# A two-layer SSD and DeltaNet trunk on one core: a list of units with three entries moved, and small weights loaded in another order

## The chip, the cores and the metric

The kernel runs on one core of one Trainium2 chip. The metric is device time in microseconds (us) of one execution, lower is better. Besides, one execution is recorded by the hardware profiler; its times are the ones that rows and views show.

The core has a matrix engine (PE, whose weight loads stand apart as PEld), a vector engine (DVE), a scalar engine for activations (ACT), GpSimd (POOL) and a queue that issues DMAs (SP). Each runs its own instructions in the order in which they stand. One waits for another through semaphores.

## The reference, cut to what matters

Two layers. Each is a SwiGLU feed-forward block at half weight, a mixing block, and a second feed-forward block; all are float32, on 256 tokens of width 1024. The mixing block is what the change touches:

```
u = rms_norm(h, mix_norm[l])
(z_s, xbc, dt_s, qkv, z_d, b_d, a_d, gate_s, gate_d) = jnp.split(u @ w_in[l], split_points, axis=-1)
y_s = mamba2_branch(z_s, xbc, dt_s, ...)        # 32 heads of 64 channels in 4 groups, chunks of 128 tokens
y_d = deltanet_branch(qkv, z_d, b_d, a_d, ...)  # 8 heads of 128 channels, chunks of 64 tokens
merged = (sigmoid(gate_s) * (y_s @ ssm_w_branch[l]) + sigmoid(gate_d) * (y_d @ dn_w_branch[l]))
h = h + merged @ w_out[l]
```

In the Mamba branch, per group of 8 heads, with `xs` the convolved and activated input, `dt` a softplus and `a_cum` a running sum of `dt * a`:

```
xdt    = xs * dt
y_diag = (C B^T * exp(a_cum[l] - a_cum[s]) * causal) @ xdt      # decay products, inside a chunk
y_off  = C @ state_in * exp(a_cum)                              # from the chunk before
yg     = (y_diag + y_off + xs * D) * silu(z)
y      = yg * rsqrt(mean(yg^2) + eps) * ssm_norm                # mean over the group's 512 channels
```

## The kernel before, in words

**Weights.** All large weights stream through one path. A slab of 128x1024 float32 (`wraw`, 5 buffers, 512 KB) is loaded by SP, rounded to a high half by ACT (`whi`, line 68) and subtracted to a low half by DVE (`wlo`, line 71); 5 buffers hold each half. Every product is three matmuls: high by high, high by low, low by high. A buffer comes free when the last matmul on it is done, so ACT's next `whi` waits for PE, and SP's next load waits for DVE's `wlo`. `take()` hands out the next slab and makes the preparations five ahead.

**The mixing block.** `mixer` computes units in the order of the list `ORDER` (line 46); the stream of weights is laid out in DRAM in the same order. `x20` is the first and `x21` the second half of the third group's input (48 matmuls of 128x256 into a PSUM bank `xs`; then a convolution: one ACT multiply and three DVE taps `ca` for each half bank, and an ACT SiLU into `xsT`). For group g, `Dg` makes the decay matrix (`dc`: a DMA, two DVE steps, an ACT exponential, a DVE multiply); `Sg`, the first part of `ssd(g)`, transposes `xsT` on PE (8 transposes into two banks `xsb`) and makes five state inputs on DVE (`xD`, `xdt` for each chunk, and `xe`); `Tg`, the second part, makes the decay products on PE (`ydb`, 64 small matmuls, and `yob`) and then on DVE adds and gates them (`xD`, `yo`, `yz`), sums squares on ACT (`jk`, into `sss`), takes the power -1/2 on POOL (`srr`) and scales `yz` on ACT. `g` units are gates (`t` banks, 128x512 matmuls). `N` is the DeltaNet branch product `branch("d", 4, ...)`: 96 matmuls of 128x512 into four banks `b`; for each pair of heads `dn_T` transposes into a bank `oT`, multiplies on DVE (`og`), and splits into `bh` (ACT) and `bl` (DVE). `o` is the first such pair, made ahead. `y` is the first transpose (`yT`) of the Mamba branch.

**PSUM.** The pool `trp` has four banks, taken in turn by `xsb`, `oT`, `ydb`, `yob`, `yT` and other short work; the pool `accp` has four, taken in turn by `xs`, `t`, `b`. Where a tile takes a bank, its first matmul waits for the last reader of the tile that had the bank before.

**The order on each engine** is made when the program is built: units are written out in the order of `ORDER`, and a scheduler places instructions of neighbouring units among one another. It is fixed from then on.

**The start of the mixing block.** While the feed-forward block ends, SP loads three small tensors: `lp` (convolution weights), `rp` (biases and decay rates) and `wsr` (weights of 48 scalar channels), and the norm vector `nw` of the next block. `wsr` is split into `wsc` on ACT and DVE; 17 matmuls on it give `psm`, which ACT copies to `smT` and PE transposes into `pst`. `ea` is an exponential of the decay rates, on ACT; it needs a table load when the table in use is another.

Of the kernel before, what the change touches and what calls it, by code (L numbers as in the profile page):

```python
# [7 lines left out]
F32 = mybir.dt.float32  # L8
F32R = mybir.dt.float32r
I32 = mybir.dt.int32  # L10
AF = mybir.ActivationFunctionType
ALU = mybir.AluOpType
# [4 lines left out]
P = 128  # L17
# [5 lines left out]
KT = D // P  # L23
# [3 lines left out]
RPW = 112  # L27
# [18 lines left out]
ORDER = """  # L46
z20 s z10 z11 s z21 s M k1 k0 q1 k2 k3 K1 K0 q3 q0 K3 K2 v0 q2 I Q0 I Q3 I z30 v1 z31 Q2 v2 V0 I v3
V1 I V3 I Q1 V2 d0 R R R b3 R b2 b0 R b1 R d2 R x00 R d1 x01 R d3 R R P R g100 g101 D0 S0 x10 T0 D1
x11 g110 g111 S1 x20 T1 o x21 N D2 y S2 D3 x30 x31 T2 g000 g010 g001 S3 g011 T3
""".split()  # L50


# [1 line left out]
def trunk_kernel(ctx, tc, x, wst, wsm, norms, lpar, rpar, cst, out):  # L54
    nc = tc.nc
    V, A, G, PE = nc.vector, nc.scalar, nc.gpsimd, nc.tensor

    cpool = ctx.enter_context(tc.tile_pool(name="cpool", bufs=1))
    wpool = ctx.enter_context(tc.tile_pool(name="wpool", bufs=1))
    slots = ctx.enter_context(tc.tile_pool(name="slots", bufs=1))  # L60
    s2 = ctx.enter_context(tc.tile_pool(name="s2", bufs=9))
# [5 lines left out]
    def act(o, i, func=AF.Copy, **kw):  # L67
        return A.activation(out=o, in_=i, func=func, **kw)  # L68

    def tt(o, a, b, op):  # L70
        return V.tensor_tensor(out=o, in0=a, in1=b, op=op)  # L71

    def stt(o, a, s, b, op0, op1):
        return V.scalar_tensor_tensor(out=o, in0=a, scalar=s, in1=b, op0=op0, op1=op1)

    def ts(o, a, s1, op0, sc2=None, op1=None):
        if op1 is None:
            return V.tensor_scalar(out=o, in0=a, scalar1=s1, scalar2=None, op0=op0)
        return V.tensor_scalar(out=o, in0=a, scalar1=s1, scalar2=sc2, op0=op0, op1=op1)
# [4 lines left out]
    def tmp2(name):  # L84
        return s2.tile([P, 512], F32, tag="s2", name=name)

    def trb(name):
        return trp.tile([P, 512], F32, tag="tr", name=name)
# [4 lines left out]
    def small(shape, name, bufs=2):  # L93
        return sm.tile(shape, F32, tag=name, name=name, bufs=bufs)
# [54 lines left out]
    state = {"loaded": 0, "prepped": 0, "taken": 0, "last": None, "hold": False, "behind": {}, "late": {}, "first": 0, "turns": {}, "first_chunk": False, "cap": n_forms}  # L149
# [62 lines left out]
    def norm_vec(i):  # L212
        nw = cpool.tile([P, D], F32, tag="nw", name="nw")
        with tc.issue_after(state["last"].ins):
            nc.sync.dma_start(nw[:], norms[i].partition_broadcast(P))
        return [nw[:, n * 512 : (n + 1) * 512] for n in range(2)]
# [375 lines left out]

    def mixer(l, nxt):
        with tc.issue_after(state["last"].ins):
            lp = cpool.tile([P, LPW], F32, tag="lp", name="lp")
            nc.sync.dma_start(lp[:], lpar[l])
            rp = cpool.tile([P, RPW], F32, tag="rp", name="rp")
            nc.sync.dma_start(rp[:], rpar[l].partition_broadcast(P))
            wsr = s2.tile([P, KT, 48], F32, tag="s2", name="wsr")
            nc.sync.dma_start(wsr[:], wsm[l])  # L600
        snw = lp[:, 240:256]
        dnw = lp[:, 256:257]
        alog = rp[:, 40:80]
# [47 lines left out]
        def scalars():  # L651
            psm = trb("psm")
            for kt in range(KT):
                both = wsc[:, kt].rearrange("p o c -> p (o c)")
                if kt < KT - 1:
                    PE.matmul(psm[0:96, 0:S], both, uTh[:, kt, :], start=kt == 0, stop=False)
                PE.matmul(psm[0:48, 0:S], wsc[:, kt, 0], uTl[:, kt, :], start=False, stop=False)
                if kt == KT - 1:
                    PE.matmul(psm[0:96, 0:S], both, uTh[:, kt, :], start=False, stop=True)
            smT = s2.tile([96, S], F32, tag="s2", name="smT")  # L660
            act(smT[:], psm[0:96, 0:S])
            pst = trb("pst")
            for t in range(2):
                PE.transpose(pst[:, t * 96 : (t + 1) * 96], smT[:, t * P : (t + 1) * P], ident[0:96, 0:96])
            pv2 = pst[:, 0:192].rearrange("p (t o c) -> p t o c", t=2, o=2)
            pvs = small([P, 2, 48], "pvs", 1)
            pv = pvs[:]
            act(pv, pv2[:, :, 1])
            tt(pv, pv2[:, :, 0], pv, ALU.add)
            scr = s2.tile([P, 5, 2, 40], F32, tag="s2", name="scr")  # L670
            xb, ax, z, s_, q_ = (scr[:, i] for i in range(5))
            tt(xb, pv[:, :, 0:40], rp[:, None, 0:40].to_broadcast([P, 2, 40]), ALU.add)
            act(dq[:, :, 8:16], pv[:, :, 40:48], AF.Tanh, scale=0.5)
            ts(dq[:, :, 8:16], dq[:, :, 8:16], 0.5, ALU.mult, 0.5, ALU.add)
            ea = small([P, 40], "ea", 1)
            with tc.issue_after(state["input"][0].ins):
                act(ea[:], alog, AF.Exp)
            stt(ax, xb, -1.0, xb, ALU.mult, ALU.max)
            act(z, ax, AF.Exp, scale=-1.0)
            ts(s_, z, 2.0, ALU.add)  # L680
            V.reciprocal(out=s_, in_=s_)
            tt(s_, s_, z, ALU.mult)
            tt(q_, s_, s_, ALU.mult)
            ts(z, q_, 1.0 / 15.0, ALU.mult)
            for d_ in (13.0, 11.0, 9.0, 7.0, 5.0, 3.0):
                stt(z, z, 1.0 / d_, q_, ALU.add, ALU.mult)
            stt(z, z, 1.0, s_, ALU.add, ALU.mult)
            ts(ax, xb, 0.0, ALU.max)
            stt(sp[:], z, 2.0, ax, ALU.mult, ALU.add)
            stt(la[:], sp[:], -1.0, ea[:, None, :].to_broadcast([P, 2, 40]), ALU.mult, ALU.mult)  # L690
            yield
            psr = trb("psr")
            for t in range(2):
                PE.matmul(psr[0:40, t * 256 : (t + 1) * 256], la[:, t, :], UU, start=True, stop=True)
            pr = psr[:].rearrange("p (t c) -> p t c", t=2)
            V.tensor_copy(rows[0:32], pr[0:32, :, 0:P])
            V.tensor_copy(rows[32:40], pr[32:40, :, P : 2 * P])
            nc.sync.dma_start(rdram[:], rows[:].rearrange("p t c -> p (t c)"))
            pac = trb("pac")
            for t in range(2):  # L700
                PE.transpose(pac[:, t * 40 : (t + 1) * 40], rows[:, t, :], ident[0:40, 0:40])
            V.tensor_copy(ac[:], pac[:, 0:80].rearrange("p (t c) -> p t c", t=2))
            V.tensor_copy(dq[:, :, 0:8], ac[:, :, 32:40])
            yield
            psp = trb("psp")
            for c in range(4):
                PE.matmul(psp[:, c * 16 : (c + 1) * 16], SEL[c % 2], dq[:, c // 2, :], start=True, stop=True)
            for a in range(2):
                V.tensor_copy(
                    pq[64 * a : 64 * a + 64].rearrange("p k h c -> p c k h"),  # L710
                    psp[64 * a : 64 * a + 64, 0:64].rearrange("p (c k h a) -> p c k h a", c=4, k=2, h=4)[:, :, :, :, a],
                )
# [484 lines left out]
        def dn_branch():  # L1197
            ps = branch("d", 4, dn_T)
            m = tg[1]
            for t in range(2):  # L1200
                for n in range(2):
                    sl = slice(n * 512, (n + 1) * 512)
                    stt(m[:, t, sl], m[:, t, sl], 1.0, ps[t][n][:], ALU.add, ALU.mult)

        sc, inv, rc = scalars(), invert(), recur()
        units = {"k": k_unit, "q": q_unit, "v": v_unit}
        rests, heads = {}, {}
# [73 lines left out]
    norm_first(nw0)  # L1281
    for l in range(DEPTH):
        ffn(norm_vec(3 * l + 1))
        mixer(l, norm_vec(3 * l + 2))
        add = ffn(norm_vec(3 * l + 3) if l + 1 < DEPTH else None)
    nw = norm_vec(3 * DEPTH)
    for t in range(2):
# [3 lines left out]
        o = tmp2("fo"), tmp2("fo")  # L1291
# [7 lines left out]
        z = small([P, 2], "zz")  # L1299
# [139 lines left out]
```

## Time and profile before

| what | us |
|---|---|
| time, median of 3 runs (1545.19 to 1546.01) | 1545.27 |
| time of the profiled execution | 1543.84 |
| its span, first to last instruction | 1542.1 |
| PE busy | 1525.1 |
| PEld busy | 1385.3 |
| DVE busy | 1229.8 |
| ACT busy | 949.8 |
| POOL busy | 82.6 |
| layer 1: `z20` to the end of the mixing block | about 202 to 594 |
| layer 2: the same | about 964 to 1355 |

A row of a timeline reads: start, duration, engine, line, operation, output and inputs, shape, count, and in brackets how long the engine had been idle and what ended that. Matmul durations are modelled and overlap, so the starts of neighbouring matmuls tell more than durations: a 128x512 matmul begins about 0.23 us after the one before, a 128x256 about 0.117 us. Rows of the chain of waits give start, duration and what. Rows of the waits give the wait's total, its number and the longest.

### The profile page before, as it was taken

To read this page: it belongs to the slowest core of one execution; us is meant where nothing else is said; L and a number is where in the kernel's file an instruction comes from. 1 tells how busy PE (TensorE), PEld (TensorE's weight loads), DVE (VectorE), ACT (ScalarE), POOL (GpSimd) and SP (SyncE) were. 2 spreads that over 40 slices of the span, in tenths; PEclk is the share of its full clock that TensorE was granted. 3 is DMA by queue.
4 is the path that set the end of the run, shared out by engine and by line. 5 is a ranking of instruction groups with operands and counts; after the bars stand their busy time and mean duration, and the time that the engine had idled before them with its cause. 6 is when DMAs were issued, how large, how long until landed. Compare 5 with 4: busy or idle time off the path is not lost.

```text
span 1542.1 us, 29082 instructions
## 1 busy us (share of the span) xinstructions
PE 1525.1 (99%) x11473; PEld 1385.3 (90%) x11473; DVE 1229.8 (80%) x1859; ACT 949.8 (62%) x1536; POOL 82.6 (5%) x92
## 2 busy tenths in 40 slices
PE   8999999999999999999999999999999999999998
PEld 7999879999988888999899998899998888899997
DVE  5878768967899766789778887689579996678886
ACT  5656667766665645566555566776756666455565
POOL 0000010000000000000100012010000000000010
PEclk9999999999999999999999999999999999999999
DMA  7687765553565556577866687566346555556775
GB/s 272 187 266 227 232 223 174 183 164 112 180 209 172 157 174 191 184 252 217 264 221 227 204 254 238 182 196 186 117 137 204 180 167 187 175 179 191 250 241 156
DMA packets 98831, 305.73 MB, mean 198 GB/s; under 512 B 22837, under 2 KB 23813, under 8 KB 97670
## 3 DMA queue, kind: packets, MB, share of 16 engines
q1 hardware_dynamic: 93796, 290.95, 57.1%
q0 software_dynamic: 4608, 12.58, 5.0%
q8 instruction: 90, 1.47, 0.4%
q14 instruction: 47, 0.39, 0.1%
q10 hardware_dynamic: 290, 0.33, 0.1%
HBM read 297.72 MB, written 1.92 MB: 194 GB/s over the span
## 4 chain that ended last, share of the span: by engine, by line
PE 90%; DVE 3%; ACT 3%; DMA 2%; issue 1%; POOL 0%; SPq 0%; POOLq 0%; ACTq 0%; DVEq 0%
PE fc L346 10%; PE fc L340 9%; PE fc L345 9%; PE t L366 9%; PE o L337 4%; PE o L336 4%; PE o L335 4%; PE f L366 3%; PE b L337 3%; PE b L335 3%; PE b L336 3%; PE p L336 2%; PE p L335 2%; PE p L337 2%; PE xs L340 1%; PE xs L345 1%
## 5 line engine op out<-in xcount | busy, mean ns | idle before, releaser
L71 DVE TENSOR_TENSOR wlo<-wraw,whi 128x1024 fp32r<-128x1024 f32 x488 | 592.2, 1222 | 189.9 <-ACT whi L68 175.4
L68 ACT ACTIVATE whi<-wraw 128x1024 fp32r<-128x1024 f32 x488 | 511.4, 1059 | 266.8 <-PE fc L345 87.3
L346 PE MATMUL fc<-uW,wlo 128*128 128x256 f32 x1280 | 354.9, 277 | 0.0
L340 PE MATMUL fc<-uW,whi 128*128 128x256 f32 x1280 | 354.1, 277 | 0.0
L345 PE MATMUL fc<-uW,whi 128*128 128x256 f32 x1260 | 348.3, 276 | 0.0
L340 PEld LDWEIGHTS fc<-uW,whi 128*128 128x128 f32 x1280 | 240.5, 188 | 0.8
L346 PEld LDWEIGHTS fc<-uW,wlo 128*128 128x128 f32 x1280 | 240.5, 188 | 0.0
L345 PEld LDWEIGHTS fc<-uW,whi 128*128 128x128 f32 x1260 | 236.5, 188 | 0.8
L366 PE MATMUL t<-whi,uW 128*128 128x512 f32 x512 | 165.4, 397 | 0.0
L366 PEld LDWEIGHTS t<-whi,uW 128*128 128x128 f32 x512 | 95.9, 188 | 21.6 <-issue 1.3
L68 ACT ACTIVATE whi<-wsum 128x1024 fp32r<-128x1024 f32 x64 | 68.0, 1062 | 58.7 <-PE fc L345 32.3
L366 PE MATMUL t<-wlo,uW 128*128 128x512 f32 x256 | 100.1, 392 | 0.0
L71 DVE TENSOR_TENSOR wlo<-wsum,whi 128x1024 fp32r<-128x1024 f32 x64 | 78.2, 1222 | 8.3 <-ACT whi L68 5.9
L335 PE MATMUL b<-whi,bh 128*128 128x512 f32 x192 | 76.1, 398 | 0.3 <-ACT bh L68 0.2
L336 PE MATMUL b<-wlo,bh 128*128 128x512 f32 x192 | 75.0, 390 | 0.0
L337 PE MATMUL b<-whi,bl 128*128 128x512 f32 x192 | 74.3, 394 | 0.3 <-DVE bl L71 0.3
L340 PE MATMUL xs<-uW,whi 128*128 128x256 f32 x256 | 72.8, 284 | 0.0
L346 PE MATMUL xs<-uW,wlo 128*128 128x256 f32 x256 | 71.4, 279 | 0.0
L345 PE MATMUL xs<-uW,whi 128*128 128x256 f32 x254 | 70.5, 278 | 0.0
L335 PE MATMUL o<-whi,gh 128*128 128x512 f32 (+1 forms) x160 | 62.0, 388 | 0.0
L337 PE MATMUL o<-whi,gl 128*128 128x512 f32 (+1 forms) x160 | 61.8, 386 | 0.0
L336 PE MATMUL o<-wlo,gh 128*128 128x512 f32 (+1 forms) x160 | 61.7, 386 | 0.0
(337 smaller groups left out, 3301.2 us busy)
## 6 DMA issues: line engine op xcount, KB each, us to landing
wraw<-in_wst_dram SPq DMA_DIRECT2D x504, 512.0 KB, 4.8
wsum<-in_wst_dram SPq DMA_DIRECT2D x16, 512.0 KB, 7.3
wsum<-in_wst_dram POOLq DMA_DIRECT2D x16, 512.0 KB, 8.6
dc<-rdram SPq DMA_DIRECT2D x8, 1024.0 KB, 8.6
nw<-in_norms_dram SPq DMA_DIRECT2D x6, 512.0 KB, 5.3
h<-u POOLq DMA_DIRECT2D x12, 256.0 KB, 6.4
gb<-rdram SPq DMA_DIRECT2D x8, 256.0 KB, 6.1
h<-in_x_dram SPq DMA_DIRECT2D x4, 256.0 KB, 3.7
```

What stands on the lines that cost most here:

```text
L68: return A.activation(out=o, in_=i, func=func, **kw)
L71: return V.tensor_tensor(out=o, in0=a, in1=b, op=op)
L335: PE.matmul(ps, lh, rh, start=start, stop=False)
L336: PE.matmul(ps, lh, rl, start=False, stop=False)
L337: return PE.matmul(ps, ll, rh, start=False, stop=stop)
L340: PE.matmul(ps, wh, mh, start=start, stop=False)
L345: PE.matmul(ps, wh, ml, start=False, stop=False)
L346: PE.matmul(ps, wl, mh, start=False, stop=stop)
L366: ins = PE.matmul(ps[t][:], st, mv, start=k0 == 0 and j == 0, stop=k0 == KT - 2 and j == 5)
```

## The change

Two places. In `ORDER` the unit `x20` moves ahead of `S1`, and `T1` moves behind `x21`; the weight stream in DRAM follows. In `mixer` the small loads change: `wsr` comes first and lies in the slot `y3` rather than in one of nine short-lived buffers, then `rp`, `lp`, and the norm vector last; and `ea` is placed behind another exponential, `z`, of the same table.

```
 ORDER = """
 ...
 V1 I V3 I Q1 V2 d0 R R R b3 R b2 b0 R b1 R d2 R x00 R d1 x01 R d3 R R P R g100 g101 D0 S0 x10 T0 D1
-x11 g110 g111 S1 x20 T1 o x21 N D2 y S2 D3 x30 x31 T2 g000 g010 g001 S3 g011 T3
+x11 g110 g111 x20 S1 o x21 T1 N D2 y S2 D3 x30 x31 T2 g000 g010 g001 S3 g011 T3
 """.split()
...
     def mixer(l, nxt):
         with tc.issue_after(state["last"].ins):
+            wsr = slots.tile([P, KT, 48], F32, tag="y3", name="wsr")
+            nc.sync.dma_start(wsr[:], wsm[l])
+            rp = cpool.tile([P, RPW], F32, tag="rp", name="rp")
+            nc.sync.dma_start(rp[:], rpar[l].partition_broadcast(P))
             lp = cpool.tile([P, LPW], F32, tag="lp", name="lp")
             nc.sync.dma_start(lp[:], lpar[l])
-            rp = cpool.tile([P, RPW], F32, tag="rp", name="rp")
-            nc.sync.dma_start(rp[:], rpar[l].partition_broadcast(P))
-            wsr = s2.tile([P, KT, 48], F32, tag="s2", name="wsr")
-            nc.sync.dma_start(wsr[:], wsm[l])
+        nxt = norm_vec(nxt)
...
             ea = small([P, 40], "ea", 1)
-            with tc.issue_after(state["input"][0].ins):
+            stt(ax, xb, -1.0, xb, ALU.mult, ALU.max)
+            with tc.issue_after(act(z, ax, AF.Exp, scale=-1.0).ins):
                 act(ea[:], alog, AF.Exp)
-            stt(ax, xb, -1.0, xb, ALU.mult, ALU.max)
-            act(z, ax, AF.Exp, scale=-1.0)
...
-        mixer(l, norm_vec(3 * l + 2))
+        mixer(l, 3 * l + 2)
```

The places that the prediction speaks of, as the instructions stand. First ACT at the start of the mixing block, before (-) and now (+):

```order
 L68 ACTIVATE uW<-hnT 128x4x128 x2
+L68 ACTIVATE wsc<-wsr 128x8x48
 L68 ACTIVATE yz<-t_2180 128x512
-L68 ACTIVATE whi<-wraw 128x1024
-L68 ACTIVATE wsc<-wsr 128x8x48
-L68 ACTIVATE whi<-wraw 128x1024
-L68 ACT_TABLE_LOAD
-L68 ACTIVATE ea<-rp 128x40
-L68 ACTIVATE whi<-wraw 128x1024
-L68 ACT_TABLE_LOAD
+L68 ACTIVATE whi<-wraw 128x1024 x3
```

The split of the small weights moved ahead of the first gate and of three roundings, and `ea` left with two table loads (it stands some rows later, behind another exponential, with none).

Second, PE in the DeltaNet branch as it stands now, from the end of the third bank's part for the first pair of heads (`oT_5620` and `oT_5667` are the third and fourth pair, `xsb_5771` group 2, `bh_5439` the first pair, `bh_5580` the second):

```order
L337 MATMUL b_5571<-whi_5347,bl_5440 128x512
L1154 MATMUL oT_5620<-cs_79,vb_2285 128x2x64 x4
L1154 MATMUL oT_5667<-cs_79,vb_2285 128x2x64 x4
L1169 MATMUL yT_5760<-cs_79,yz_2179 128x128 x4
L335 MATMUL b_5572<-whi_5341,bh_5439 128x512
L336 MATMUL b_5572<-wlo_5342,bh_5439 128x512
L337 MATMUL b_5572<-whi_5341,bl_5440 128x512
L335 MATMUL b_5572<-whi_5347,bh_5439 128x512
L336 MATMUL b_5572<-wlo_5348,bh_5439 128x512
L337 MATMUL b_5572<-whi_5347,bl_5440 128x512
L1101 MATMUL xsb_5771<-cs_79,xsT_5337 128x128 x4
L335 MATMUL b_5569<-whi_5446,bh_5580 128x512
```

Before, at the end of the same branch:

```order
L335 MATMUL b_5572<-whi_5639,bh_5674 128x512
L336 MATMUL b_5572<-wlo_5640,bh_5674 128x512
L337 MATMUL b_5572<-whi_5639,bl_5675 128x512
L1169 MATMUL yT_5760<-cs_79,yz_2179 128x128 x3
L1101 MATMUL xsb_5771<-cs_79,xsT_5357 128x128 x4
L1101 MATMUL xsb_5780<-cs_79,xsT_5357 128x128 x4
```

So the transposes `xsb` of group 2 stood behind all 96 matmuls of this branch; now four of them stand after the first 24. By the turn of the four banks, `xsb_5771` takes the bank that `oT_5573` (the second pair) had, whose reader is `og_5578`.

Third, ACT and DVE at that time. ACT before:

```order
L68 ACTIVATE bh_5492<-og_5490 128x512
L68 ACTIVATE xsT_5357<-ca_5426 128x256
L68 ACTIVATE yz_2398<-yz_2398,srr_5481 128x512 x2
L68 ACTIVATE whi_5586<-wraw_5359 128x1024
L68 ACTIVATE bh_5580<-og_5578 128x512
```

ACT now:

```order
L68 ACTIVATE jk_5562,sss_5557<-yz_2398 128x512
L68 ACTIVATE whi_5592<-wraw_5345 128x1024
L68 ACTIVATE yz_2398<-yz_2398,srr_5565 128x512 x2
L68 ACTIVATE bh_5580<-og_5578 128x512
L68 ACTIVATE whi_5633<-wraw_5444 128x1024
```

and DVE now:

```order
L71 TENSOR_TENSOR yz_2398<-yz_2398,xD_5417 128x512
L71 TENSOR_TENSOR yz_2398<-yz_2398,xD_5426 128x512
L71 TENSOR_TENSOR wlo_5587<-wraw_5339,whi_5586 128x1024
L79 TENSOR_SCALAR sss_5557<-sss_5557 128x2
L74 SCALAR_TENSOR_TENSOR og_5578<-oT_5573,lp_2175,zdT_4029 128x512
L71 TENSOR_TENSOR wlo_5593<-wraw_5345,whi_5592 128x1024
```

The sum of squares, its power and the scaling of group 1's output, all of `T1`, now stand ahead of `og_5578` on DVE and of `bh_5580` on ACT. Before, all of `T1`'s adds and gates on DVE stood ahead of the first pair's `og` (`og_5490`), with only `sss` behind it; ACT's scaling `yz` stood between `bh` of the first pair (`bh_5492`) and `bh_5580`, with one rounding `whi_5586` behind it. Now, between the two pairs' `bh` on ACT, there stand a table load, seven rows of `x20`'s second half and `x21`, two roundings, both sums `jk` and the scaling.

## The prediction

> **What bounds the kernel now.** I read the engines' shares first, then the chain of waits, then what PE waits for, then the stage that the change touches.
>
> ```profile
> span 1542.1 us, 29082 instructions
> PE 1525.1 (99%) x11473; PEld 1385.3 (90%) x11473; DVE 1229.8 (80%) x1859; ACT 949.8 (62%) x1536; POOL 82.6 (5%) x92
> PE 90%; DVE 3%; ACT 3%; DMA 2%; issue 1%; POOL 0%; SPq 0%; POOLq 0%; ACTq 0%; DVEq 0%
> ```
>
> PE is busy for 99% of the span and is 90% of the chain that ended last. No matmul is added or removed, so the time moves only by what PE waits: a wait removed is a gain, a new one a loss. The other engines count only where PE waits for them. The waits of PE, and those of its weight loads, which reach the same waits a little sooner, that bear on the change:
>
> ```profile
> PE xsb L1101 <- ACT xsT L68: 1.7, 2, 0.9
> PE pst L664 <- ACT smT L68: 0.5, 1, 0.5
> PE b L337 <- DVE bl L71: 0.3, 1, 0.3
> PE b L335 <- ACT bh L68: 0.2, 1, 0.2
> PEld xsb L1101 <- ACT xsT L68: 2.1, 2, 1.1
> PEld pst L664 <- ACT smT L68: 1.1, 2, 0.9
> PEld b L335 <- ACT bh L68: 1.0, 3, 0.4
> PEld b L337 <- DVE bl L71: 0.7, 1, 0.7
> ```
>
> The first four sum to 2.7 us, the last four to 4.9. Of the stage where units move, the windows tell how full the other engines are (after the length: PE, PEld, DVE, ACT, POOL):
>
> ```profile
> 440.00:475.00 35.00, 33.58 (x259) 28.87 (x259) 33.51 (x46) 23.50 (x35) 2.21 (x1) 1.00 0.49 158
> ```
>
> From 440 to 475 DVE (the third engine) is busy for 33.51 of 35 us, PE for 33.58. So here two engines are full together, and the change reorders both. The second layer has the same rows some 762 us later.
>
> **The change part by part: what it removes.** Each layer's `S1` transposes waited for `xsT`, the SiLU of `x11`'s end:
>
> ```profile
> 444.83 0.28 PE L345 MATMUL xs<-uW,whi 128*128 128x256 f32 x1
> 446.04 0.44 PE L1101 MATMUL xsb<-cs,xsT 128*128 128x128 f32 x2 [0.93 <-ACT xsT L68]
> ```
>
> From start to start this is 1.21 us where 0.12 would do, so 1.1 us (0.9 in layer 2). Now all 48 matmuls of `x20` stand ahead, over 5 us of work, and `xsT` is long there: this goes. `bh` and `bl` of the first pair were late by some 0.3 and 0.5 us by such gaps. Now they are made under `x21`'s matmuls, so this goes as well. The small weights take the wait for `smT` (0.6, and about 0.2 in layer 2). The gaps sum to 3.8 us, between the bounds of 2.7 and 4.9; I take 3.8.
>
> **The small weights.** The rows at the start of the first layer's mixing block:
>
> ```profile
> 192.88 0.42 SPq L596 DMA_DIRECT2D lp<-in_lpar_dram  x1
> 195.68 0.38 SPq L600 DMA_DIRECT2D wsr<-in_wsm_dram  x1
> wsr<-in_wsm_dram SPq DMA_DIRECT2D x1, 192.0 KB, 6.1
> 201.84 0.53 ACT L68 ACTIVATE wsc<-wsr 128x384 fp32r<-128x384 f32 x1 [2.42 <-DMA wsr<-in_wsm_dram]
> 203.33 1.28 ACT L68 ACT_TABLE_LOAD   x1
> ```
>
> `wsr` is now issued first, at about 192.9, and lands by 199.0 at its 6.1 us, 2.8 us sooner. ACT then has no 2.42 us of idling in front of `wsc`, and `ea` behind another exponential saves two table loads of 1.28 each, so that `smT` comes sooner and PE's wait at `pst` ends. `wsc` stands ahead of a gate and a rounding that before ran at 196.94 and 198.37. If `wsr` were late, they would be late; `z20`'s matmuls on them begin near 202, so 3 us of other work cover it. I take 0 for this, with 0 to 1 us for both layers together. On SP's queue `lp` and `rp` move behind `wsr`, and `nw` behind them all; `lp` is first needed for a convolution near 238, over 40 us later; `nw` waits for DVE as before.
>
> **What it adds.** Without the wait, PE starts `x20` at 442.56 and I walk on with these rows:
>
> ```profile
> 442.56 0.82 PE L1101 MATMUL xsb<-cs,xsT 128*128 128x128 f32 x6
> 450.29 2.08 PE L1115 MATMUL ydb<-xdt,dc 128*64 128x64 f32 x64
> 452.30 1.12 PE L1121 MATMUL yob<-xe,cbt 128*128 128x512 f32 x2
> 453.26 0.60 PE L1154 MATMUL oT<-cs,vb 128*128 128x128 f32 x4
> 459.16 1.25 PE L1154 MATMUL oT<-cs,vb 128*128 128x128 f32 x10
> 467.48 0.24 PE b L336
> ```
>
> Before, four transposes (0.36) and the 48 matmuls of `x21` stood between the rows of 453.26 and 459.16: 5.54, or 0.115 each. So `x20` takes 5.5, to 448.1; eight transposes 0.8, to 448.9; `oT` 0.4; `x21` 5.5, to 454.8; `ydb` 2.0 and `yob` 0.95 (by their starts), to 457.8; `oT_5573` 0.4; then 18 `b` matmuls at 0.23, to 462.3; twelve short transposes, 1.1, to 463.4; six more `b`, 1.4. By its own work PE reaches `xsb_5771` at about 464.8, and the second pair's first `b_5569` 0.4 later, at 465.2.
>
> DVE cannot follow. From the first `xsb` (448.8) to the end of `og_5578`, which frees the bank that `xsb_5771` takes, the order holds 11 steps on 128x512, 4 `wlo`, 12 taps, 2 `og`, one `bl` and the small `sss`. Their prices by starts:
>
> ```profile
> 446.52 0.69 DVE L71 TENSOR_TENSOR xD<-xsb,rp 128x512 f32<-128x512 f32 x1
> 447.12 0.68 DVE L71 TENSOR_TENSOR xdt<-xsb,sp 128x512 f32<-128x512 f32 x1
> 458.64 0.74 DVE L74 SCALAR_TENSOR_TENSOR og<-oT,lp,zdT 128x512 f32<-128x512 f32 x1
> 459.29 0.47 DVE L74 SCALAR_TENSOR_TENSOR ca<-xs,lp,ca 128x253 f32<-128x253 f32 x1
> 459.68 0.16 DVE L79 TENSOR_SCALAR sss<-sss 128x2 f32<-128x2 f32 x1
> 459.75 1.22 DVE L71 TENSOR_TENSOR wlo<-wraw,whi 128x1024 fp32r<-128x1024 f32 x1
> 460.88 0.69 DVE L71 TENSOR_TENSOR bl<-og,bh 128x512 fp32r<-128x512 f32 x1
> 461.49 0.48 DVE L74 SCALAR_TENSOR_TENSOR ca<-xs,lp,ca 128x255 f32<-128x255 f32 x1
> ```
>
> That is 0.60 for a step, 0.65 for `og`, 0.39 for a tap, 0.07 for `sss`, 1.13 for `wlo`, 0.61 for `bl`: 6.6 + 4.5 + 4.7 + 1.3 + 0.6 + 0.1 = 17.8, so `og_5578` ends near 466.6. PE is there at 464.8 and waits 1.8. The last tap of `x21` already holds `b_5572` (it takes the bank of `x21`'s `xs`) by about 0.5 of this; together I take 2.0, with 1.7 to 2.3 by the uncertainty of the walk. What is queued behind `xsb_5771` on PE is all the rest of the branch, so nothing else fills the wait.
>
> Then `b_5569` needs `bh_5580` on ACT. ACT's order puts `T1`'s scaling `yz` ahead of it, and that waits for POOL's power of `sss`:
>
> ```profile
> 459.92 2.21 POOL L210 TENSOR_TENSOR srr<-sss,mhalf 128x2 f32<-128x2 f32 x1 [25.59 <-DVE sss L79]
> 462.16 1.34 ACT L68 ACTIVATE yz<-yz,srr 128x512 f32<-128x512 f32 x2 [1.32 <-POOL srr L210]
> 463.40 1.04 ACT L68 ACTIVATE whi<-wraw 128x1024 fp32r<-128x1024 f32 x1
> 464.35 0.61 ACT L68 ACTIVATE bh<-og 128x512 fp32r<-128x512 f32 x1
> 1222.41 1.61 POOL L210 TENSOR_TENSOR srr<-sss,mhalf 128x2 f32<-128x2 f32 x1 [25.77 <-DVE sss L79]
> ```
>
> `sss` ends 0.65 ahead of `og`, at 466.0. POOL takes 0.2 to begin and 1.6 (layer 2's row; layer 1's took 2.21), to 467.8; `yz` twice, 1.24, to 469.1; `bh` 0.61, to 469.75. PE, through the first wait and its four transposes, is ready at 467.2 and goes on at 469.8: 2.6 us more, 3.2 with the slow power, and nothing if the scaling were not in the way. Behind `bh_5580` nothing is late next: the raw slabs are loaded before, and ACT and DVE then work ahead of the 72 remaining `b` matmuls, 16 us.
>
> The sum: 2 layers x (2.0 + 2.6) = 9.2 added, 3.8 removed, net +5.4. Against the profiled execution's 1543.84 (span 1542.1 and 1.74 around it) that is 1549.2; the median of the runs stands 1.4 above the profiled execution, so **1550.7** for the median.
>
> A table load now stands directly in front of `x20`'s second half on ACT, and the next row tells its price:
>
> ```profile
> 455.04 1.28 ACT L68 ACT_TABLE_LOAD   x1
> 456.34 0.42 ACT L68 ACTIVATE xsT<-ca 128x256 f32<-128x256 f32 x1
> ```
>
> The SiLU starts 0.02 behind the load's end, so a switch costs 1.28. The Trainium skill, ScalarE: Activation LUTs, section What ACT_TABLE_LOAD costs, says that a drain of about 1380 ns comes on top of the load for every switch of set, 2.66 us in all. By that rule, if the drain stood behind the load, `ca_5406` and DVE's taps would be some 1.1 us later in each layer and the sum would be +7.6; the trace shows 0.02 and not 1.38, and the measurement decides.
>
> **The rivals.** *Faster.* If DVE and ACT need about 2 us less up to `og_5578`, and the scaling is over 4 us sooner than I walk, only the removed waits count: 1545.27 - 3.8 = 1541.5. For it: before, the same steps of `T1` cost PE less than 1 us at the branch. Against it: then PE had `x21` behind `T1`, 5.5 us of cover, which now stands ahead of it; and DVE's 33.51 of 35 leaves 1.5 us, not 4.
>
> *No change.* If ACT has `bh_5580` in time, and only the bank holds PE, the sum is 2 x 2.0 - 3.8 = +0.2: 1545.5. This needs `sss` at least 2.6 us sooner, where DVE has no idle time to give.
>
> *Worse.* If POOL's power takes 2.21 in both layers the sum is +6.6: 1551.9. With the upper bound of 2.3 for the first wait, that power and only 2.7 removed, it is 2 x 5.5 - 2.7 = +8.3: 1553.6. If `wsr` comes late, up to 1 more.
>
> *The Trainium skill's drain.* By 1.1 in each layer, 1552.9; the row above speaks against it, so 0.03.
>
> **How the numbers follow.** What a measurement of this kernel can tell from no change is about 0.2%, 3.1 us: 1542.2 to 1548.4. My forecast with its bounds, slower, has 0.55, the worse cases beside it 0.22 and the drain 0.03: slower 0.80. No change has 0.12, faster 0.08; the faster case wants DVE and the POOL chain both to be early. The likeliest case alone spans 1548.6 (2 x 4.1 with 4.9 removed) to 1553.5. The range, with no more than 2 in 10 left out, reaches down to the case of no change: 1545.4 to 1553.5.
>
> **What would show it.** In the changed kernel's waits of PE there should be `xsb` held by DVE's `og`, about 1.5 us, twice; `b` at L335 held by ACT's `bh`, about 2.6, twice; `b` held by DVE's `ca`, about 0.5, twice. The waits of `xsb` for `xsT` and of `pst` for `smT` should be gone, and four table loads fewer on ACT. DVE should have no idle time from the first `xsb` of `S1` to `og_5578`. I am wrong if `og_5578` ends within 16 us of that `xsb`, if POOL's power starts well ahead of `og_5578`'s end, or if a new wait stands in the feed-forward block or at `z20`, where I price the small weights at nothing.

## The result, and the profile after

| | median, us | runs |
|---|---|---|
| before, beside it | 1545.39 | 12 (1544.36 to 1548.76) |
| changed | 1549.43 | 12 (1546.40 to 1550.53) |

The ratio is 1.0022 with a 95% interval of 1.0015 to 1.0030: slower by 3.4 us (2.3 to 4.6); by the medians 4.0. The prediction was 1550.7, slower, in a range of 1545.4 to 1553.5. The profiled execution of the changed kernel took 1548.87 us.

The head of its page:

```profile
span 1546.8 us, 29086 instructions
PE 1525.6 (99%) x11473; PEld 1386.9 (90%) x11473; DVE 1229.5 (79%) x1859; ACT 944.9 (61%) x1532; POOL 80.0 (5%) x92
```

The same window as before, whose columns are length, then busy time of PE, PEld, DVE, ACT and POOL:

```profile
440.00:475.00 35.00, 32.33 (x258) 28.25 (x257) 33.57 (x47) 23.66 (x35) 0.69 (x1) 1.00 0.57 181
```

The span is 4.7 longer while PE's work is the same: PE waited more. In the window PE does 32.33 rather than 33.58, and DVE is as full as it was. PE's longest waits now:

```profile
PE hnT L282 <- DVE hn L74: 3.1, 2, 1.7
PE b L335 <- ACT bh L68: 2.7, 2, 1.4
PE xsb L1101 <- DVE og L74: 2.6, 2, 1.3
PE nw L245 <- DMA row<-in_norms_dram: 2.3, 1, 2.3
PE cbb L1045 <- DVE vb L71: 2.2, 2, 1.4
```

The waits of `xsb` for `xsT`, of `pst` for `smT` and of the first pair's `b` are gone. Two new ones stand there: `xsb` for `og` and `b` for `bh`, twice each. Here they are in the timeline of PE, with DVE, POOL and ACT beside them (rows of four engines, each in its own order):

```profile
465.53 0.40 PE L337 MATMUL b<-whi,bl 128*128 128x512 f32 x1
467.24 0.66 PE L1101 MATMUL xsb<-cs,xsT 128*128 128x128 f32 x4 [1.32 <-DVE og L74]
469.25 0.50 PE L335 MATMUL b<-whi,bh 128*128 128x512 f32 x1 [1.35 <-ACT bh L68]
...
466.38 0.16 DVE L79 TENSOR_SCALAR sss<-sss 128x2 f32<-128x2 f32 x1
466.45 0.74 DVE L74 SCALAR_TENSOR_TENSOR og<-oT,lp,zdT 128x512 f32<-128x512 f32 x1
467.13 1.23 DVE L71 TENSOR_TENSOR wlo<-wraw,whi 128x1024 fp32r<-128x1024 f32 x1
...
466.61 0.69 POOL L210 TENSOR_TENSOR srr<-sss,mhalf 128x2 f32<-128x2 f32 x1 [32.15 <-DVE sss L79]
...
467.34 1.34 ACT L68 ACTIVATE yz<-yz,srr 128x512 f32<-128x512 f32 x2 [0.24 <-POOL srr L210]
468.58 0.61 ACT L68 ACTIVATE bh<-og 128x512 fp32r<-128x512 f32 x1
```

The last `b` of the first pair starts at 465.53 and would let the transposes start at 465.76. They start at 467.24, as `og` ends: 1.48 us. They need 0.4; `b` then starts at 469.25 as `bh` ends: 1.6 more. On ACT `bh` stands behind both scalings `yz`, and these wait for POOL's power. Layer 2 has the same rows with the same waits.

In layer 2 something else follows the wait. Windows of 4 us; the third number from the end is the clock granted to PE:

```profile
1228.00:1232.00 4.00, 2.13 (x11) 1.28 (x9) 4.00 (x7) 3.57 (x8) 0.69 (x1) 1.00 0.28 84
1232.00:1236.00 4.00, 3.20 (x8) 2.58 (x9) 4.00 (x4) 2.29 (x4) 0.00 (x0) 0.57 0.63 203
1236.00:1240.00 4.00, 4.00 (x19) 3.25 (x19) 4.00 (x5) 1.47 (x3) 0.00 (x0) 1.00 0.41 132
```

For about 3.4 us ((1 - 0.57) x 4 / 0.5) PE was granted half its clock, from inside the second wait on. By the gaps of starts the 72 matmuls of `b` that follow took 1.2 us longer than the same 72 in layer 1 (17.8 against 16.6). The kernel before shows no such stretch, except at its very end (1536 to 1540), where PE does nothing.

This is not the profiled execution alone. Over a whole run such a stretch lowers the mean granted clock by about 0.001 (0.5 x 3.4 of 1547 us). Of the 12 runs of the changed kernel 11 have a mean clock of 0.997 or 0.998 and take 1547.8 to 1550.5 us; the one with 0.999 took 1546.40, only 1.0 above the median before. Of the 29 runs of the kernel before that stand beside the first experiments, 25 have 0.999 or more. So a part of the loss, perhaps much of it, goes with the half clock that follows the waits; one run at the higher clock is too few to say how much.

### The profile page after: what moved, and what is told of

It is laid out like the page before. It is cut to its first block, busy times and chain, and to the rows that moved or that the text cites. A ratio compares the mean times of both kernels' runs of the same rounds, so it can differ in the third digit from the quotient of the medians.

```text
span 1546.8 us, 29086 instructions
## 1 busy us (share of the span) xinstructions
PE 1525.6 (99%) x11473; PEld 1386.9 (90%) x11473; DVE 1229.5 (79%) x1859; ACT 944.9 (61%) x1532; POOL 80.0 (5%) x92
```

## The experiments

Each ratio is against runs of the kernel before on the same chip, whose medians were 1544.65 for the first four, 1545.71 for the next four and 1545.28 for the last four. e1_order_only has 6 runs, e6_t1_after_n 4, the others 9 to 12. A ratio need not be the quotient of the medians (e3_scale_late: 1.0012 and 1.0021), so differences under 0.1% between two versions are not read here.

| run | median, us | ratio | 95% interval |
|---|---|---|---|
| e1_order_only | 1551.07 | 1.0037 | 1.0023 to 1.0050 |
| e2_small_only | 1543.46 | 0.9990 | 0.9982 to 0.9999 |
| e3_scale_late | 1547.82 | 1.0012 | 1.0003 to 1.0022 |
| e4_t1_back | 1542.90 | 0.9987 | 0.9978 to 0.9996 |
| e5_pair_first | 1543.69 | 0.9984 | 0.9975 to 0.9993 |
| e8_pair_early | 1543.48 | 0.9988 | 0.9979 to 0.9997 |
| e6_t1_after_n | 1552.40 | 1.0040 | 1.0026 to 1.0054 |
| e9_ea_only | 1543.04 | 0.9977 | 0.9968 to 0.9986 |
| e10_pair_ea | 1544.28 | 0.9985 | 0.9976 to 0.9995 |
| e11_dma_only | 1544.79 | 0.9994 | 0.9984 to 1.0004 |
| e12_small_again | 1543.16 | 0.9984 | 0.9974 to 0.9994 |
| e13_ea_again | 1543.14 | 0.9980 | 0.9969 to 0.9990 |

### The two parts of the change

e1_order_only is the kernel before with one line of the change:

```
-x11 g110 g111 S1 x20 T1 o x21 N D2 y S2 D3 x30 x31 T2 g000 g010 g001 S3 g011 T3
+x11 g110 g111 x20 S1 o x21 T1 N D2 y S2 D3 x30 x31 T2 g000 g010 g001 S3 g011 T3
```

> The order of units as changed, the small weights and ea as before. If the new waits in the DeltaNet branch are the whole cost, xsb still waits 1.5 us for og and b 1.6 us for bh in each layer, and the time is that of the changed kernel, 1549.4 within 0.7: what the small weights saved at pst (0.6) was given back at cbb, which waits for DVE's vb. If the small weights are worth what they save at pst, the time is 1550.2. If they cost something elsewhere, it is under 1548.5.

e2_small_only is the changed kernel with that line as before:

> The small weights and ea as changed, the order of units as before. The wait at pst goes, 0.6 us in layer 1. If it is given back, cbb waits about 1.4 us for vb rather than 0.5 and the time is 1545.4 within 0.5. If it is kept, 1544.6. A cost of the small weights would show as over 1546.

The order alone costs 0.37%, 5.7 us (3.6 to 7.7); the small weights alone gain 0.1 to 0.2% (a second time, below, 0.9984). So the order is the loss, and the small weights cover a part of it. Against my expectation for e1_order_only the time stands even above the 1550.2 of the case that the small weights keep what they save. The waits of e1_order_only are the same two and a larger one at `pst`; in layer 2 a half clock follows that lasts twice as long. Its waits view:

```profile
PE b L335 <- ACT bh L68: 2.7, 2, 1.4
PE xsb L1101 <- DVE og L74: 2.6, 2, 1.3
PE pst L664 <- ACT smT L68: 1.2, 1, 1.2
```

and in windows of 4 us, as above:

```profile
1232.00:1236.00 4.00, 2.65 (x9) 2.02 (x10) 4.00 (x4) 2.80 (x4) 0.03 (x1) 0.66 0.71 223
1236.00:1240.00 4.00, 4.00 (x11) 3.14 (x10) 4.00 (x5) 0.63 (x1) 0.00 (x0) 0.50 0.40 109
```

My expectation that `cbb` takes back all that `pst` saved was wrong. In e2_small_only PE's wait at `cbb` was 0.87 us in layer 1, against 0.46 before; in the changed kernel 1.45. What ends it is a DMA: `vb` stands on DVE behind the first step on `dc`. The next fence has that step in the kernel before, the one after it in the changed kernel:

```profile
403.38 2.29 DVE L71 TENSOR_TENSOR dc<-dc,ac 128x2048 f32<-128x2048 f32 x1 [0.64 <-DMA dc<-rdram]
```

```profile
403.52 2.29 DVE L71 TENSOR_TENSOR dc<-dc,ac 128x2048 f32<-128x2048 f32 x1 [1.63 <-DMA dc<-rdram]
```

In e2_small_only it starts at 402.99, though the instructions up to there are those of the changed kernel: the landing of this DMA differs by half a microsecond and more from one execution to the next, and it takes back a varying part of what PE gained ahead of it.

### Which of the moved units

e3_scale_late is the changed kernel, with the power and the scaling of `T1` as a step `U1` of its own, behind `N`:

```
-x11 g110 g111 x20 S1 o x21 T1 N D2 ...
+x11 g110 g111 x20 S1 o x21 T1 N U1 D2 ...
             ts(ss[:], ss[:], 1.0 / 512.0, ALU.mult, EPS, ALU.add)
+            yield
             rr = small([P, 2], "srr")
```

> The changed kernel, with T1's power (POOL) and scaling (ACT) put behind N; all else stays. If the scaling in front of bh holds PE, the wait for bh falls from 1.6 us to 0.4 or less, that for og at xsb stays at 1.5, and with PE idle for less than 2 us at a time the halved clock after it should not come: 1549.4 - 2.4 - up to 1.5, so 1545.5 to 1547. If DVE alone sets it, the time stays at 1549.

The wait for `og` stayed, and the one for `bh` fell from 1.35 to 0.71 by the waits as the profile has them, from 1.6 to 1.0 by the starts in which the expectation is written:

```profile
467.13 0.66 PE L1101 MATMUL xsb<-cs,xsT 128*128 128x128 f32 x4 [1.32 <-DVE og L74]
468.50 0.50 PE L335 MATMUL b<-whi,bh 128*128 128x512 f32 x1 [0.71 <-ACT bh L68]
...
465.94 1.99 ACT L68 ACTIVATE whi<-wraw 128x1024 fp32r<-128x1024 f32 x2
467.83 0.61 ACT L68 ACTIVATE bh<-og 128x512 fp32r<-128x512 f32 x1
468.35 1.32 ACT L68 ACTIVATE yz<-yz,srr 128x512 f32<-128x512 f32 x2
```

`bh` now starts 0.75 sooner than in the changed kernel, but a second rounding `whi` came ahead of it. So the scaling held `bh`, as the prediction has it; with it gone the rounding does, and the run does not tell what the scaling alone costs. The time was above what I expected: less was gained, and the half clock came in layer 2 all the same (0.98 from 1228 to 1232, 0.59 from 1232 to 1236), behind waits of less than 2 us each. Again it is not in every run: the 4 of 12 with a mean clock of 0.999 took 1545.8 us on the average, within the range expected, and the 8 with a lower one 1548.0.

e4_t1_back is the changed kernel with `T1` ahead of `x21` again:

```
-x11 g110 g111 x20 S1 o x21 T1 N D2 ...
+x11 g110 g111 x20 S1 o T1 x21 N D2 ...
```

> The changed kernel with T1 ahead of x21 again; x20 stays ahead of S1. If T1's place makes the cost, the waits for og and bh in the branch go; PE then waits for xe at yob, by about 1.2 us in each layer, since only 16 matmuls stand between: 1545.4 - 3.8 + 2.4 = 1544, within 1. If x20's place makes it, since DVE starts on S1 later, the waits stay and the time is near 1549.

The wait for `og` is gone, `bh` holds PE by 0.7 in each layer, and the expected wait at `yob` did not come: some `x21` matmuls were placed between the decay products and cover it. The ratio is 0.9987 where the changed kernel has 1.0022, 5.4 us less by the ratios, and no stretch at half clock is left. So it is `T1`'s place, not `x20`'s, that costs.

e5_pair_first leaves `T1` behind `x21` but takes the second pair of heads ahead of it, as a unit `p`:

```
-x11 g110 g111 x20 S1 o x21 T1 N D2 ...
+x11 g110 g111 x20 S1 o x21 p T1 N D2 ...
+            elif kind == "p":
+                dn_T(1)
-            ps = branch("d", 4, dn_T)
+            ps = branch("d", 4, dn_T, made=2)
```

> The changed kernel with the second pair's transposes and og ahead of T1 on PE and DVE (the branch makes its third and fourth pair as before). If og and bh of the second pair behind T1's tail make the cost, both waits go (at most 0.5 us is left in each layer), the transposes xsb ahead of S1 still wait for nothing, and the time is 2.5 to 4 us below the kernel before. If DVE's whole load between S1 and the branch makes it, the wait only moves to the third pair's bh, and the time stays 2 us or more above the kernel before.

e8_pair_early puts the same unit ahead of `x21`:

```
+x11 g110 g111 x20 S1 o p x21 T1 N D2 ...
```

> The changed kernel with the second pair ahead of x21 already, behind the first. By the place of og and bh: as with the pair behind x21, 2.5 to 4 us below the kernel before. By DVE's whole load: 2 us or more above it. The taps of x20 come later on DVE for it; if they hold PE, it shows at xsb of group 2.

Both waits are gone in both, with nothing taken out of the computation and `T1` where the change put it. The time goes from 0.22% above to 0.16% and 0.12% below the kernel before: 2.5 and 1.9 us, at the edge of the 2.5 to 4 expected and under it. The waits view of e5_pair_first has a new row in return:

```profile
PE t L366 <- DVE wlo L71: 1.5, 2, 0.8
```

So the cause is where `og` and `bh` of the second pair stand against `T1`'s tail. One thing moved along: the turn of the banks shifts by a pair, so that in e5_pair_first group 2's `xsb` stands behind some 48 matmuls of the branch (470.95) and no longer behind 24; for the wait at `xsb` the run does not tell an earlier `og` from a later `xsb`. In e4_t1_back, where `xsb` stands behind 18 (465.74), an earlier `og` is enough. The rival, DVE's whole load, keeps a part: freed from this wait, PE meets DVE's backlog 40 us later, at the gates (508.03 in layer 1).

All of the gain is no more than what the small weights gain with the old order (0.9990 and 0.9984), and these runs hold the small weights as well. That the mended order is worth anything by itself is not shown.

e6_t1_after_n puts `T1` behind `N`:

```
+x11 g110 g111 x20 S1 o x21 N T1 D2 ...
```

> The changed kernel with T1 behind N in the list, so that its decay products stand among and behind the branch's matmuls. By the place of og and bh behind T1: no wait in the branch, 2 to 4 us below the kernel before, unless group 2's S2, which needs the buffers of xD and xdt that T1 then still holds, makes PE wait at xsb or x30 instead: up to 2 us back. By DVE's whole load: no better than the changed kernel.

A miss: no faster than the changed kernel, as the rival has it, and the slowest by its median (4 runs). The branch does run without a wait, but `T1`'s work is pushed onto group 2's, and PE waits for DVE at the gates, not at `xsb` or `x30` for buffers:

```profile
505.71 0.47 PE L366 MATMUL t<-whi,uW 128*128 128x512 f32 x1 [2.17 <-DVE ca L74]
...
1269.29 0.44 PE L1101 MATMUL xsb<-cs,xsT 128*128 128x128 f32 x2 [1.17 <-ACT xsT L68]
1271.98 0.76 PE L366 MATMUL t<-whi,uW 128*128 128x512 f32 x1 [2.25 <-DVE ca L74]
```

Here both layers have a stretch at half clock behind the wait (in layer 1 0.80 and 0.78 from 504 to 512; in layer 2 0.87, 0.50 and 0.78 from 1268 to 1280).

### The small weights

e9_ea_only is the kernel before with only `ea` moved; e13_ea_again is the same once more:

```
-            with tc.issue_after(state["input"][0].ins):
-                act(ea[:], alog, AF.Exp)
             stt(ax, xb, -1.0, xb, ALU.mult, ALU.max)
-            act(z, ax, AF.Exp, scale=-1.0)
+            with tc.issue_after(act(z, ax, AF.Exp, scale=-1.0).ins):
+                act(ea[:], alog, AF.Exp)
```

> The kernel before with only ea moved behind the other exponential: the DMAs of wsr, rp, lp and the norm vector in the old order. Two table loads go from ACT in each layer. If these make the wait at pst, it falls from 0.5 to under 0.2 and the time is 0.5 to 1.2 below the kernel before, as with the whole of the small weights' change. If the late wsr makes it, pst still waits and the time is the kernel before's within 0.5.

> Only ea moved, again, on the same chip as the DMA order by itself and both together: 0.5 to 2.7 us below the kernel before (the 2.7 of the first time was more than pst's 0.5 to 0.7 and two table loads less on ACT in each layer can explain, so nearer to 1). If it stays at 2.7, the table loads held PE at more places than pst.

e11_dma_only has the small DMAs and the slot of `wsr` as changed, and `ea` as before; e12_small_again has both parts:

> The kernel before with only the four small DMAs in the new order and wsr in the slot y3; ea in its old place. If the table loads of ea make the wait at pst, wsc runs some 5 us sooner but pst still waits 0.4 to 1.2 us and the time is the kernel before's within 0.7. If the late wsr made the wait, pst waits for nothing and the time is 0.5 to 1.2 us less.

> Both parts of the small weights' change again, units as before, beside the two parts by themselves on one chip. If only ea matters, this is 0.5 to 2 us below the kernel before, as ea by itself within 0.7. If the DMA order costs, it is 1 us or more above ea by itself.

`ea` alone gives what both give (0.9980 and 0.9984 on one chip), and the DMAs alone are not told from no change. Yet in the profile of e11_dma_only `pst` waits for nothing either. The rows of ACT up to `smT` tell why, first in e1_order_only (`smT` at 211.06 and `pst` held by 1.25), then in e11_dma_only, then in e9_ea_only:

```profile
202.44 0.53 ACT L68 ACTIVATE wsc<-wsr 128x384 fp32r<-128x384 f32 x1 [3.20 <-DMA wsr<-in_wsm_dram]
...
211.06 0.37 ACT L68 ACTIVATE smT<-psm 96x256 f32<-96x256 f32 x1
```

```profile
196.03 0.53 ACT L68 ACTIVATE wsc<-wsr 128x384 fp32r<-128x384 f32 x1 [0.26 <-DMA wsr<-in_wsm_dram]
196.57 1.28 ACT L68 ACT_TABLE_LOAD   x1
...
208.93 0.38 ACT L68 ACTIVATE smT<-psm 96x256 f32<-96x256 f32 x1 [0.78 <-PE psm L660]
```

```profile
202.61 0.53 ACT L68 ACTIVATE wsc<-wsr 128x384 fp32r<-128x384 f32 x1 [3.30 <-DMA wsr<-in_wsm_dram]
...
209.65 0.38 ACT L68 ACTIVATE smT<-psm 96x256 f32<-96x256 f32 x1 [0.78 <-PE psm L659]
```

A late `wsr` and two table loads together make ACT late: with the table loads early (e11_dma_only) or gone (e9_ea_only, where `wsr` was as late as in e1_order_only) `smT` waits for its own matmuls alone, and PE does not wait at `pst`. In the kernel before the wait was 0.5 us with `wsc` at 201.84, in e1_order_only 1.25 with `wsc` at 202.44, so it varies from execution to execution. That `ea` by itself measures 2 us and more, while the profiled waits at `pst` are 0.5 to 1.2, is not explained. The profiled executions do not show it (spans of 1541.6 in e9_ea_only and 1543.6 in e13_ea_again, 1542.1 before). Why the DMAs by themselves measure less, though they remove the same wait, stays open too (the intervals of the two overlap).

e10_pair_ea puts the two parts that gained together:

> The second pair's og ahead of T1, as in the run before with it, and of the small weights' change only ea moved (DMAs in the old order). If the DMA order is worth nothing, 2 to 4 us below the kernel before and a profile without waits for og, bh or smT. If the early wsr is needed once x20 stands early, the pst wait or one at z20 comes back and the gain is under 2 us.

By the ratio it is 2.3 us faster than the kernel before (0.9985), as expected, and its profile has no wait for `og`, `bh` or `smT`; but it is not faster than `ea` alone. No version measured less than the simplest, the kernel before with `ea` moved (0.9977 and 0.9980), though the intervals of all the faster ones overlap.

## Why the prediction was right

**The bound.** PE's busy time stayed (1525.1 and 1525.6), and the span moved by PE's waits.

**What is removed.** All as forecast: `xsb` for `xsT` (1.1 and 0.9), the first pair's `bh` and `bl` (0.3 and 0.5), `pst` (0.6 and 0.2). These terms come to 3.6, not to the 3.8 that the prediction writes for their sum. The part at `pst` is one execution's, and some of it is given back at `cbb`.

**The walk to `og`.** DVE was to work without a gap from the first `xsb` for 17.8 us. It started at 449.31 and `og` ended as the next instruction began, at 467.13: 17.8, with no idle time in between. The size of the wait was taken as 2.0, with 0.5 of it at `b_5572` for the last tap. That part did not come: the taps ended at 464.04 and PE came at 464.29. What stood at `xsb` was 1.48, the 1.5 that was forecast there. The length of DVE's work was right; that the wait met its forecast so closely is in part luck. PE came to `xsb` at 465.76 rather than 464.8 (`x20` began 0.3 later than walked, and `x20` and `x21` took 5.8 and 5.6, not 5.5 each), `og` ended 0.5 later than walked, and the half microsecond at the tap was not there.

**The wait for `bh`.** The chain is the one forecast: `sss`, power, two scalings, `bh`. It was 1.6 and not 2.6 by the starts, and this is the term that was most mis-sized: "POOL takes 0.2 to begin and 1.6". It began after 0.07 and took 0.69. The two differences make 1.0, the whole error. I took the duration from a row of before without asking what DVE did beside it (below).

**The sum.** Added were 2 x 3.1 = 6.2 and not 9.2; 1.2 came on top from the half clock in layer 2, which I had not foreseen; 3.6 went. That is +3.8, and the profiled spans differ by 4.7. The rest is of the size of other waits that differ between the two profiles: `cbb` 2.2 against 1.3, `hnT` 3.1 against 2.5. So the two waits stand where the prediction has them, but that the total came out 1.3 us too high and not more is in part luck: 3.0 too much in the two waits was partly made up by a half clock that no term of the sum holds. It may also be that without this clock the loss would not have been clear of noise: the one run at 0.999 lies below the 1548.4 up to which the prediction counts a time as no change.

**The small weights.** Priced at the wait of `pst`, 0.8 for both layers, and nothing else. `wsr` was there by 196.5 (`wsc` began at 196.48, 4.2 after the issue at 192.29), not at 199.0, and nothing at `z20` waited for it. The wait at `pst` went; measured by time, this part was worth more, 1.5 to 3.6 us by the ratios of the four runs that hold `ea`'s move and the old order, of which the profile shows half at most.

**The rivals.** "Faster" fell by the two waits; that it needed DVE early was right. "No change" needed the scaling not to hold `bh`; in e3_scale_late it did not, and a rounding held `bh` in its place. The slow power did not come: 0.69 in both layers. The table load in front of `xsT` cost 1.28 (455.76 to 457.05), and no drain stood behind it.

## What to carry to other kernels

A list of units that is moved takes its tail along: what counted was not the unit's matmuls but its work on the other engines, the adds and gates that came to stand ahead of the next unit's `og` on DVE, and one power and two scalings ahead of its `bh` on ACT. Where an engine is full for 18 us (DVE here), count its steps up to the instruction that PE needs; that count came out to 0.1 us. And a small operation moved off the path (`ea`, two table loads in each layer) measured as much here as any reordering around it, though the profile shows only a part of that gain.

## What the runs showed of the hardware

**POOL's power depends on what DVE does.** The operation on 128x2 is the same everywhere. In e4_t1_back `sss` is followed by a `wlo`, and the power takes 1.61; in the changed kernel `og` follows, and it takes 0.69 (shown above):

```profile
463.01 0.17 DVE L79 TENSOR_SCALAR sss<-sss 128x2 f32<-128x2 f32 x1 [0.21 <-ACT jk L68]
463.09 1.23 DVE L71 TENSOR_TENSOR wlo<-wraw,whi 128x1024 fp32r<-128x1024 f32 x1
...
463.26 1.61 POOL L210 TENSOR_TENSOR srr<-sss,mhalf 128x2 f32<-128x2 f32 x1 [28.03 <-DVE sss L79]
```

With two `wlo` behind `sss`, as for group 2 in e5_pair_first, it takes 2.74:

```profile
508.35 2.36 DVE L71 TENSOR_TENSOR wlo<-wraw,whi 128x1024 fp32r<-128x1024 f32 x2
...
508.52 2.74 POOL L210 TENSOR_TENSOR srr<-sss,mhalf 128x2 f32<-128x2 f32 x1 [38.57 <-DVE sss L79]
```

These are roughly 0.7 and what is left of DVE's `wlo`, which has both inputs in SBUF, when POOL begins (about 1.0 of one, 2.1 of two). `og` reads one of its inputs from PSUM. In the kernel before, `wlo` and then `bl` followed in both layers; it took 2.21 in layer 1, as if it had waited for both, but 1.61 in layer 2, as for `wlo` alone. Why is open. The Trainium skill, GPSIMD Engine Reference, Specifications, says that GpSimd shares its SBUF interfaces with VectorE and that VectorE's instructions with two SBUF inputs contend with it; the rows agree but for that one, and no run here isolates it.

**PE's clock after a wait.** Behind two waits of together 2.5 to 3.1 us PE ran at half clock for 3.4 us (e3_scale_late, changed kernel) or for twice that (6.7 in e1_order_only, (0.34 x 4 + 0.50 x 4) / 0.5; 6.8 in layer 2 of e6_t1_after_n, by the three windows given there); behind a single wait of 2.2 us in layer 1 of e6_t1_after_n for 3.4 ((0.20 x 4 + 0.22 x 4) / 0.5). It was seen in layer 2 of four kernels and in layer 1 only of e6_t1_after_n, though in the other three the waits of the two layers agree; why is open. The Trainium skill, TensorE: Matmul & The Clock Gate, What's actually happening, gives a free-running window of about 3.4 us and a half clock behind a whole idle one. The length agrees. That a whole window must be idle does not: in the changed kernel PE was busy for 2.13 of 4 us between 1228 and 1232, and its longest wait without a matmul was 1.6 us.
